# A wider pad beside right-hand tiles, a second raw weight buffer in the up projections, and modulation pieces in halves over eight slabs

## The chip, the cores and the metric

One core of a Trainium2 chip runs one program. The metric is the device time of the program in microseconds (us).

## What is computed

Two transformer blocks in float32 on 1024 tokens of width 1024. The first has a gated delta rule and a latent attention, the second a short convolution and a stick-breaking attention, whose inputs are modulated by a vector. Both end in a feed-forward part with 4096 hidden columns. What the change touches, from the reference:

```
h = rms_norm(x, ffn_pre_norm[l])
f = jnp.square(jax.nn.relu(h @ w_up[l])) @ w_down[l]
x = x + rms_norm(f, ffn_post_norm[l])
...
mod = c @ w_ada[l] + b_ada[l]
sh1, sc1, gt1, sh2, sc2, gt2 = jnp.split(mod, N_MOD, axis=-1)
h = modulate(rms_norm_2(x, g_pre_mix[l]), sh1, sc1)
proj = h @ w_in[l]
...
h2 = modulate(rms_norm_2(x, g_pre_mlp[l]), sh2, sc2)
ff = jnp.square(jax.nn.relu(h2 @ w_mlp_in[l])) @ w_mlp_out[l]
```

## The kernel before

Every product is made of three matmuls per contraction tile of 128: each operand is split into a high part (rounded, `w_hi`, made by ScalarE) and a low part (`w_lo`, the rest, made by VectorE), and high times high, high times low and low times high are summed in PSUM.

**The up projection** (`up_stage`, `ffn_up`, L1039) runs once per block, and is called stage 1 and stage 2 here. It works on 16 slabs of 256 hidden columns. A slab is a 2 by 2 block product in a form with seven products in place of eight; a product is 12 matmuls of 512 columns. The moving operand is a tile of activations, the stationary one a piece of weights. Two of the seven products use the activation quarters `hq` (left-hand tiles); the other five use `hq_t`, five tiles made from sums of quarters, which lie on the right-hand side of the memory. For the first 12 slabs (`LEAD`) the two `hq` products are made ahead, while the activations are still being normed, and parked in DRAM (`fx_dr`), so that such a lead slab has 5 products, 60 matmuls; the last four slabs have 84.

In a slab (L1060) SP loads 1 MB of weights into `w_raw`; it is the only buffer for raw weights, and the other stages use it too. VectorE makes four sums of weight quarters (`fws`, L1070), ScalarE and VectorE split `fws` and quarters of `w_raw` into two sets of `w_hi` and `w_lo` (L178, L179); there are two buffers of each, so both are in use in every slab. VectorE takes the products out of PSUM (L1095 to L1122: `fu2`, `fu3`, `f00`, `f11`, `f01`, `f10`), ScalarE squares them after a relu (L1050, L1051), VectorE makes five sums of the squares (`fs`, L1127, three buffers), and SP writes them to DRAM (L1043). ScalarE's queue writes two more. What `fs` holds is read back by the down projection.

**The modulation** (L1226 to L1277) computes `c @ w_ada` on VectorE in pieces of 512 columns: four loads of 512 KB on POOL's queue, two VectorE instructions for each (`ada_acc`, L1235 and L1237). Four pieces are worked off in stage 1, one `yield` per slab (`side(c)`), eight more in the first part of block 2.

**Memory.** Tiles with `side="right"` are stacked from the right-hand end. `edge` (L1512) is a pad, a tile that nothing uses, put there before `hq_t` (`between`, L1529) and before `h`, the activations of block 2 (L1561 to L1563). The right-hand end that the program may use lies 32 bytes below a multiple of 256 bytes. The addresses in this and the next section are those of the built programs.

The order of instructions on each engine comes from a scheduler; within `ffn_up` the products ahead have a high priority (L1131). An engine's instructions, and the DMAs of its queue, start in their order.

Of the kernel before, what the change touches and what calls it, by code (L numbers as in the profile page):

```python
# [8 lines left out]
F32 = mybir.dt.float32  # L9
# [8 lines left out]
P = 128  # L18
# [15 lines left out]
TAGS = {  # L34
# [5 lines left out]
}  # L40
# [25 lines left out]
def tile_two_blocks(ctx: ExitStack, tc: tile.TileContext, I, out):  # L66
# [5 lines left out]
    wp = ctx.enter_context(tc.tile_pool(name="wp", bufs=2))  # L72
# [966 lines left out]
    def ffn_up(hq, w_up, fl, fp, first, side):  # L1039
# [18 lines left out]
            return x  # L1058

        def slab(c, lead):  # L1060
            raw = wp.tile([P, 2112], F32, name="w_raw", tag="w_raw", bufs=1)[:, :2048]
            SP.dma_start(raw.rearrange("p (k n) -> p k n", k=8),
                         w_up[:, 256 * c:256 * c + 256].rearrange("(k p) n -> p k n", p=P))
            r4 = raw.rearrange("p (h k i n) -> p h i k n", h=2, k=4, i=2)
            (a11, a21), (a12, a22) = ([r4[:, h, i] for i in range(2)] for h in range(2))
            ws = fp.tile([P, 4, 4, P], F32, name="fws")
            s2, s3, s1, s4 = (ws[:, n] for n in range(4))
            for o, x, z, op in ((s1, a21, a22, ALU.add), (s2, s1, a11, ALU.subtract), (s3, a11, a21, ALU.subtract),
                                (s4, a12, s2, ALU.subtract)):
                DVE.tensor_tensor(out=o, in0=x, in1=z, op=op)  # L1070
            u = [[wp.tile([P, 2112], F32R, name=nm, tag=nm)[:, :2048].rearrange("p (s k n) -> p s k n", s=4, k=4)
                  for nm in ("w_hi", "w_lo")] for _ in range(2)]

            def halves_of(t, slots, v):
                split(t[0][:, slots], t[1][:, slots], v)

            def op(t, n):
                return [x[:, n] for x in t]

            if not lead:  # L1080
                halves_of(u[0], slice(2, 4), r4[:, :, 0])
            halves_of(u[0], slice(0, 2), ws[:, 0:2])
            halves_of(u[1], slice(0, 2), ws[:, 2:4])
            halves_of(u[1], 2, a22)
            if lead:
                x, f11 = (fp.tile([P, 512], F32, name=nm) for nm in ("fx", "f00"))
                for i, t in enumerate((x, f11)):
                    SP.dma_start(t, fx_dr[:, 512 * (2 * c + i):512 * (2 * c + i) + 512])
                q2 = f11
            else:  # L1090
                x = p1(fp, op(u[0], 2))
            q6 = mm_tile()
            product(q6, op(u[0], 0), "t2")
            u2 = fp.tile([P, 512], F32, name="fu2")
            DVE.tensor_tensor(out=u2, in0=x, in1=q6, op=ALU.add)  # L1095
            if not lead:
                q2 = mm_tile()
                product(q2, op(u[0], 3), "b21")
                f11 = fp.tile([P, 512], F32, name="f00")
            DVE.tensor_tensor(out=f11, in0=x, in1=q2, op=ALU.add)  # L1100
            square(f11)
            left(c, 2, f11, ACT)
            q7 = mm_tile()
            product(q7, op(u[0], 1), "t3")
            u3 = fp.tile([P, 512], F32, name="fu3")
            DVE.tensor_tensor(out=u3, in0=u2, in1=q7, op=ALU.add)
            q5 = mm_tile()
            product(q5, op(u[1], 0), "t1")
            f22 = fp.tile([P, 512], F32, name="f11")
            DVE.tensor_tensor(out=f22, in0=u3, in1=q5, op=ALU.add)  # L1110
            square(f22)
            left(c, 3, f22, ACT)
            q4 = mm_tile()
            product(q4, op(u[1], 2), "t4")
            f12 = fp.tile([P, 512], F32, name="f01")
            DVE.tensor_tensor(out=f12, in0=u3, in1=q4, op=ALU.subtract)
            square(f12)
            f21 = fp.tile([P, 512], F32, name="f10")
            DVE.tensor_tensor(out=f21, in0=u2, in1=q5, op=ALU.add)
            q3 = mm_tile()  # L1120
            product(q3, op(u[1], 1), "b22")
            DVE.tensor_tensor(out=f21, in0=f21, in1=q3, op=ALU.add)  # L1122
            square(f21)
            for i, x, z, o in ((4, f11, f12, ALU.add), (0, f11, f22, ALU.add), (6, f12, f22, ALU.subtract),
                               (1, f21, f22, ALU.add), (5, f21, f11, ALU.subtract)):
                t = fp.tile([P, 512], F32, name="fs")
                DVE.tensor_tensor(out=t, in0=x, in1=z, op=o)  # L1127
                left(c, i, t)


        with tc.high_priority(offset=100):  # L1131
            for c in range(LEAD):
# [3 lines left out]
                for i, (a, b) in enumerate(((a11, "b11"), (a12, "b21"))):  # L1136
                    acc = mm_tile()
# [85 lines left out]
        return res  # L1223


    def modulation_acc(i, pool):  # L1226

        acc = pool.tile([P, 512], F32, name="ada_acc")
        for q in range(4):
            raw = pool.tile([P, 2, 512], F32, name="ada_raw")  # L1230
            POOL.dma_start(raw, I["w_ada_2"][0][256 * q:256 * q + 256, 512 * i:512 * i + 512]
                           .rearrange("(k p) n -> p k n", p=P))
            for k in range(2):
                if q + k == 0:
                    DVE.tensor_scalar(acc, raw[:, 0, :], col(R_C), None, ALU.mult)  # L1235
                else:
                    DVE.scalar_tensor_tensor(out=acc, in0=raw[:, k, :], scalar=col(R_C + 2 * q + k), in1=acc,  # L1237
                                             op0=ALU.mult, op1=ALU.add)
        return acc

    def modulation_sum(i, acc, pool):
        row = pool.tile([P, 512], F32, name="f_r")[0:1, :]
        p = mm_tile()
        PE.matmul(p[0:1, :], ones[:, 0:1], acc, start=True, stop=True)
        ACT.copy(row, p[0:1, :])
        SP.dma_start(mod_raw[i // 2:i // 2 + 1, (i % 2) * 512:(i % 2) * 512 + 512], row)
# [18 lines left out]

    def modulation(pool, m0, m1):

        pend = None
        for i in range(2 * m0, 2 * m1):
            acc = modulation_acc(i, pool)  # L1270
            if pend is not None:
                modulation_sum(i - 1, pend, pool)
            pend = acc
            yield
        modulation_sum(2 * m1 - 1, pend, pool)
        modulation_columns(pool, m0, m1)
        yield  # L1277

# [176 lines left out]
    with sbuf("gc", 1) as gc:  # L1455
# [4 lines left out]
        with sbuf("hT1", 1) as hp:  # L1460
# [6 lines left out]
            right = ExitStack()  # L1467
# [43 lines left out]

    def edge(es, name):  # L1512

        es.enter_context(tc.tile_pool(name=name, bufs=1, side="right")).tile([P, 8], F32, name=name)

    def up_stage(n, w_out, src, mxp, mx_es, w_up, epi, tags, gains, side=lambda fp: lambda c: None):

# [24 lines left out]
    with ExitStack():  # L1542
        with banks(mm=6, tr=2):
# [7 lines left out]
            def side1(fp):  # L1551
# [7 lines left out]
                    t, xt, xn, junk, None, None, row=rows["grow"], tmp_pool=ep, put=put), spare=False),  # L1559
# [76 lines left out]
```

## Time and profile before

| | |
|---|---|
| median of 3 runs | 2800.58 us (2790.0 to 2802.42) |
| profiled execution | 2799.73 us, of which the span from its first to its last instruction is 2798.0 us |
| TensorE, share of the span with a matmul in flight | 95% |
| VectorE / ScalarE / GpSimd busy | 70% / 47% / 20% |
| TensorE clock granted, mean over the span | 0.985 |

Times within the execution are us from the span's start. Stage 1's slabs run from about 728 to 1010, stage 2's from about 2190 to 2455. A matmul of 512 columns is shown as lasting 0.39 us, but a new one starts about every 0.23 us, so the busy share of TensorE hides short waits; start times and counts show them.

### The profile page before, as it was taken

Reading aid. Unit: us, or ns where it says so; the run is one execution under the profiler, and the core shown is the slowest. Engines: PE = TensorE matmul, PEld = TensorE weight load, DVE = VectorE, ACT = ScalarE, POOL = GpSimd, SP = SyncE. Lnnn points to the kernel's source line nnn. Section 1 sums busy time; section 2 is a strip of 40 time slices with the busy share of each in tenths; the row PEclk is TensorE's granted clock in tenths of the full one; section 3 lists DMA queues with packets and bytes.
Section 4 is the critical chain, followed back from the end, with each engine's and each line's share of the span. In section 5 each row is a group of like instructions: output and inputs, shape, how many; then the busy total and the mean of one; then the engine's idle time right before and its main releaser. Section 6 shows DMA issues by size and latency. Waiting matters only on the chain. (4 is left out here: it accounts for less than half of the span.)

```text
span 2798.0 us, 39356 instructions
## 1 busy us (share of the span) xinstructions
PE 2658.9 (95%) x13801; PEld 2223.7 (79%) x13801; DVE 1957.6 (70%) x3614; ACT 1310.8 (47%) x2360; POOL 561.4 (20%) x568
## 2 busy tenths in 40 slices
PE   7899989999989999999999999998999989999996
PEld 7788879999766778777887788887798767878785
DVE  7668789858888765577765248777567778755566
ACT  4554666546544444344521146554268544443342
POOL 1242344300000022434211012111200000023412
PEclk9999999999999999999999999999999999999998
DMA  4286476356676587777574445343856566587785
GB/s 131 79 280 206 159 212 180 110 162 207 231 257 204 179 289 235 256 255 263 188 244 156 158 151 162 114 121 130 261 174 210 202 213 208 186 288 261 257 283 176
DMA packets 381500, 562.23 MB, mean 201 GB/s; under 512 B 39427, under 2 KB 215658, under 8 KB 381302
## 3 DMA queue, kind: packets, MB, share of 16 engines
q1 hardware_dynamic: 358262, 505.17, 55.0%
q10 hardware_dynamic: 16128, 29.37, 2.8%
q0 software_dynamic: 6912, 25.17, 2.8%
q8 instruction: 109, 1.79, 0.3%
q14 instruction: 89, 0.73, 0.1%
HBM read 408.83 MB, written 150.78 MB: 200 GB/s over the span
## 5 line engine op out<-in xcount | busy, mean ns | idle before, releaser
L173 PE MATMUL mm<-w_hi,df 128*128 128x512 f32 x1792 | 561.7, 394 | 13.8 <-ACT y L1197 5.7
L173 PE MATMUL mm<-hq_t,w_hi 128*128 128x512 f32 x1280 | 400.1, 401 | 26.3 <-ACT w_hi L178 24.0
L173 PEld LDWEIGHTS mm<-w_hi,df 128*128 128x128 f32 x1792 | 339.9, 190 | 88.7 <-ACT w_hi L178 7.3
L173 PE MATMUL mm<-w_lo,df 128*128 128x512 f32 x896 | 354.0, 395 | 10.9 <-DVE w_lo L179 10.8
L173 PEld LDWEIGHTS mm<-hq_t,w_hi 128*128 128x128 f32 x1280 | 240.3, 190 | 96.0 <-ACT w_hi L178 35.7
L173 PE MATMUL mm<-h_hi,w_hi 128*128 128x512 f32 x736 | 293.6, 399 | 0.0
L173 PE MATMUL mm<-h_lo,w_hi 128*128 128x512 f32 x736 | 292.4, 397 | 0.0
L173 PE MATMUL mm<-h_hi,w_lo 128*128 128x512 f32 x736 | 291.8, 397 | 0.0
L1170 POOL TENSOR_TENSOR dwr<-dwr 128x1024 f32<-128x1024 f32 x40 | 101.3, 2533 | 889.3 <-DMA dwr<-in_w_mlp_out 581.8
L173 PE MATMUL mm<-hq_t,w_lo 128*128 128x512 f32 x640 | 243.7, 398 | 8.1 <-DVE w_lo L179 8.0
L209 DVE TENSOR_TENSOR w_lo<-w_raw,w_hi 128x1024 fp32r<-128x1024 f32 (+1 forms) x138 | 170.7, 1259 | 92.7 <-ACT w_hi L203 91.7
L179 DVE TENSOR_TENSOR df<-dfr,df 128x1024 fp32r<-128x1024 f32 x112 | 155.3, 1397 | 85.3 <-ACT df L178 85.1
L203 ACT CAST w_hi<-w_raw 128x1024 fp32r<-128x1024 f32 (+1 forms) x138 | 138.8, 1047 | 158.1 <-PE mm L173 62.6
L173 PEld LDWEIGHTS mm<-w_lo,df 128*128 128x128 f32 x896 | 170.5, 190 | 51.9 <-DVE w_lo L179 16.7
L173 PE MATMUL mm<-w_hi,mixT 128*128 128x256 f32 x1024 | 183.5, 281 | 4.7 <-DVE m_sg L1439 2.0
L178 ACT CAST df<-dfr 128x1024 fp32r<-128x1024 f32 x112 | 116.5, 1051 | 120.3 <-PE mm L173 74.0
L179 DVE TENSOR_TENSOR w_lo<-dwr,w_hi 128x1024 fp32r<-128x1024 f32 x56 | 102.1, 1824 | 100.3 <-ACT w_hi L178 100.0
L173 PEld LDWEIGHTS mm<-h_hi,w_hi 128*128 128x128 f32 x736 | 138.3, 188 | 36.2 <-issue 6.3
L173 PEld LDWEIGHTS mm<-h_hi,w_lo 128*128 128x128 f32 x736 | 138.4, 188 | 29.7
L173 PEld LDWEIGHTS mm<-w_hi,mixT 128*128 128x128 f32 x1024 | 156.5, 188 | 6.7 <-ACT w_hi L203 4.0
L173 PEld LDWEIGHTS mm<-h_lo,w_hi 128*128 128x128 f32 x736 | 138.5, 188 | 29.1 <-issue 0.2
L173 PE MATMUL mm<-hq,w_hi 128*128 128x512 f32 x512 | 158.8, 391 | 0.0
(406 smaller groups left out, 5809.4 us busy)
## 6 DMA issues: line engine op xcount, KB each, us to landing
dfr<-fs SPq DMA_DIRECT2D x112, 512.0 KB
fs<-fs SPq DMA_DIRECT2D x160, 256.0 KB
w_raw<-in_w_in SPq DMA_DIRECT2D x32, 1024.0 KB
ada_raw<-in_w_ada POOLq DMA_DIRECT2D x48, 512.0 KB, 5.3
dwr<-in_w_down SPq DMA_DIRECT2D x48, 512.0 KB
w_raw<-in_w_down SPq DMA_DIRECT2D x48, 512.0 KB
dwr<-in_w_mlp_out SPq DMA_DIRECT2D x48, 512.0 KB
w_raw<-in_w_mlp_out SPq DMA_DIRECT2D x48, 512.0 KB
```

The costliest lines, as they stand in the source:

```text
L173: PE.matmul(ps, l, r, start=first and n == 0, stop=final and n == last)
L178: ACT.copy(hi, src)
L179: DVE.tensor_tensor(out=lo, in0=src, in1=r32(hi), op=ALU.subtract)
L203: ins = ACT.copy(wh[:, step * i:step * i + step], raw[:, step * i:step * i + step])
L209: DVE.tensor_tensor(out=wl[:, c], in0=raw[:, c], in1=r32(wh[:, c]), op=ALU.subtract)
L1170: POOL.tensor_tensor(out=a, in0=a, in1=b, op=ALU.subtract if sub else ALU.add)
```

## The change

`edge` becomes 224 bytes in place of 32. `hq_t` starts at byte 147200 in place of 147392, `h` of block 2 at 163584 in place of 163776: multiples of 256, where it was 192 bytes more than one. The tiles `hq`, `w_hi`, `w_lo` and block 1's `h` start at multiples of 256 in both kernels.

Odd slabs load their weights into a new tile `fraw`, even ones into `w_raw`. To make room for its 8 KB, `f01` and `f10` go: the results are made in place of `fu3` and `fu2`. `fs` has two buffers in place of three, `ada_raw` one in place of two in stage 1, `ada_acc` two in place of one. (The modulation of block 2 has pools of its own, as before.)

A piece of the modulation yields after its second load as well, and there the sum over partitions of the piece before is made. So a slab of stage 1 has half a piece, and four pieces take eight slabs; in block 2 half a piece goes with each call.

```
-    "fp": "fws fx*2 f00*2 fu2 fu3 f01 f10 f11 fs*3 ada_acc ada_raw*2 f_r",
+    "fp": "fws fraw fx*2 f00*2 fu2 fu3 f11 fs*2 ada_acc*2 ada_raw f_r",
...
         def slab(c, lead):
-            raw = wp.tile([P, 2112], F32, name="w_raw", tag="w_raw", bufs=1)[:, :2048]
+            if c % 2:
+                raw = fp.tile([P, 2048], F32, name="fraw")
+            else:
+                raw = wp.tile([P, 2112], F32, name="w_raw", tag="w_raw", bufs=1)[:, :2048]
...
-            f12 = fp.tile([P, 512], F32, name="f01")
+            f12 = u3
...
-            f21 = fp.tile([P, 512], F32, name="f10")
+            f21 = u2
...
-    def modulation_acc(i, pool):
+    def modulation_acc(i, pool, first, prev):
...
+            if q == 1:
+                if i > first:
+                    modulation_sum(i - 1, prev, pool)
+                yield
         return acc
...
         for i in range(2 * m0, 2 * m1):
-            acc = modulation_acc(i, pool)
-            if pend is not None:
-                modulation_sum(i - 1, pend, pool)
-            pend = acc
+            acc = yield from modulation_acc(i, pool, 2 * m0, acc)
             yield
...
-        es.enter_context(tc.tile_pool(name=name, bufs=1, side="right")).tile([P, 8], F32, name=name)
+        es.enter_context(tc.tile_pool(name=name, bufs=1, side="right")).tile([P, 56], F32, name=name)
```

Lines from L1062 on move by 3 to 7 (L1070 is L1073, L1127 is L1130, and so on).

The order that the scheduler makes also moves. First SP's queue at the start of stage 2's slabs, before:

```order
L1062 DMA w_raw_22739<-in_w_mlp_in_2 128x8x256
L1088 DMA f00_22757<-fx_dr_98 128x512
L1088 DMA f00_22880<-fx_dr_98 128x512
L1062 DMA w_raw_22862<-in_w_mlp_in_2 128x8x256
L1088 DMA fx_23002<-fx_dr_98 128x512
L1043 DMA fs0_99<-fs_22850 128x512
L1062 DMA w_raw_22985<-in_w_mlp_in_2 128x8x256
```

and now:

```order
L1065 DMA w_raw_22693<-in_w_mlp_in_2 128x8x256
L1065 DMA fraw_22814<-in_w_mlp_in_2 128x8x256
L1065 DMA w_raw_22935<-in_w_mlp_in_2 128x8x256
L1091 DMA fx_22952<-fx_dr_98 128x512
L1043 DMA fs0_99<-fs_22802 128x512
L1065 DMA fraw_23056<-in_w_mlp_in_2 128x8x256
L1043 DMA fs4_103<-fs_22799 128x512
```

The load for the second slab follows the first at once, and each later load stands a slab earlier than it did.

Then VectorE in a lead slab of stage 2 (`mm` is a product in PSUM), before:

```order
L1095 TENSOR_TENSOR fu2_23142<-fx_23125,mm_23129 128x512
L1127 TENSOR_TENSOR fs_23093<-f00_23003,f01_23071 128x512
L1127 TENSOR_TENSOR fs_23099<-f01_23071,f11_23053 128x512
L1127 TENSOR_TENSOR fs_23105<-f10_23075,f00_23003 128x512
L1106 TENSOR_TENSOR fu3_23161<-fu2_23142,mm_23148 128x512
L1070 TENSOR_TENSOR fws_23233<-w_raw_23231 128x512 x2
L1070 TENSOR_TENSOR fws_23233<-fws_23233,w_raw_23231 128x512
L1070 TENSOR_TENSOR fws_23233<-w_raw_23231,fws_23233 128x512
L1127 TENSOR_TENSOR fs_23102<-f10_23075,f11_23053 128x512
```

and now:

```order
L1130 TENSOR_TENSOR fs_23044<-f00_22953,f11_23003 128x512
L1130 TENSOR_TENSOR fs_23041<-f00_22953,fu3_22988 128x512
L1130 TENSOR_TENSOR fs_23050<-fu2_22969,f11_23003 128x512
L1130 TENSOR_TENSOR fs_23047<-fu3_22988,f11_23003 128x512
L179 TENSOR_TENSOR w_lo_23187<-fws_23179,w_hi_23186 128x1024
L179 TENSOR_TENSOR w_lo_23187<-w_raw_23177,w_hi_23186 128x512
L1073 TENSOR_TENSOR fws_23300<-fraw_23298 128x512 x2
L1130 TENSOR_TENSOR fs_23053<-fu2_22969,f00_22953 128x512
```

Four of the five sums follow each other, on two buffers, and the fifth comes after four instructions on weights; the weights of the next slab are worked on right behind those of this one.

Last, VectorE in a slab of stage 1 with the modulation, now:

```order
L1130 TENSOR_TENSOR fs_9994<-f00_9903,f11_9953 128x512
L179 TENSOR_TENSOR w_lo_10157<-fws_10151,w_hi_10156 128x1024
L1130 TENSOR_TENSOR fs_9991<-f00_9903,fu3_9938 128x512
L1240 SCALAR_TENSOR_TENSOR ada_acc_10006<-ada_raw_10145,vec_107,ada_acc_10006 128x512
L1130 TENSOR_TENSOR fs_10000<-fu2_9919,f11_9953 128x512
L1240 SCALAR_TENSOR_TENSOR ada_acc_10006<-ada_raw_10145,vec_107,ada_acc_10006 128x512
L1130 TENSOR_TENSOR fs_9997<-fu3_9938,f11_9953 128x512
L179 TENSOR_TENSOR w_lo_10159<-fws_10151,w_hi_10158 128x1024
L179 TENSOR_TENSOR w_lo_10159<-w_raw_10149,w_hi_10158 128x512
L1130 TENSOR_TENSOR fs_10003<-fu2_9919,f00_9903 128x512
```

The two L1240 are the halves of one load. Four instructions on the modulation fall to a slab, where a slab with a piece had eight; they and `w_lo` now stand between the sums.

## Rows read from the trace of the kernel before

**Rows 1.** The page's first part: busy us of the span, instructions.
```profile
PE 2658.9 (95%) x13801; PEld 2223.7 (79%) x13801; DVE 1957.6 (70%) x3614; ACT 1310.8 (47%) x2360; POOL 561.4 (20%) x568
```

**Rows 2.** Windows: stretch, us, busy by engine (count), PEclk, DMA share, GB/s.
```profile
728.00:867.00 139.00, 121.22 (x473) 88.83 (x472) 113.00 (x171) 55.92 (x86) 11.77 (x16) 0.95 0.69 230
867.00:927.00 60.00, 57.02 (x240) 44.26 (x239) 51.78 (x79) 28.86 (x44) 0.00 (x0) 1.00 0.68 220
927.00:1010.00 83.00, 83.00 (x358) 66.68 (x357) 59.41 (x85) 37.55 (x54) 4.10 (x2) 1.00 0.55 189
2190.00:2376.00 186.00, 172.41 (x721) 133.87 (x721) 145.82 (x219) 81.73 (x127) 0.00 (x0) 1.00 0.63 208
2376.00:2455.00 79.00, 79.00 (x343) 63.78 (x342) 58.71 (x82) 38.80 (x57) 5.24 (x3) 1.00 0.56 193
1380.00:1890.00 510.00, 508.95 (x2588) 420.65 (x2586) 312.56 (x507) 203.82 (x412) 77.56 (x152) 1.00 0.50 160
```

**Rows 3.** Waits in 2190 to 2376: us in total, times, longest.
```profile
DVE fws L1070 <- DMA w_raw<-in_w_mlp_in: 38.2, 12, 3.8
PE mm L173 <- ACT w_hi L178: 9.3, 10, 1.6
```

**Rows 4.** Timeline of one slab of stage 2: start, us, instruction, idle before.
```profile
2222.52 0.68 DVE L179 TENSOR_TENSOR w_lo<-w_raw,w_hi 128x512 fp32r<-128x512 f32 x1
2223.23 0.38 SPq L1062 DMA_DIRECT2D w_raw<-in_w_mlp_in  x1
2229.66 1.29 DVE L1070 TENSOR_TENSOR fws<-w_raw 128x512 f32<-128x512 f32 x2 [3.46 <-DMA w_raw<-in_w_mlp_in]
2231.64 1.06 ACT L178 CAST w_hi<-fws 128x1024 fp32r<-128x1024 f32 x1 [8.01 <-DVE fws L1070]
2233.88 1.21 DVE L179 TENSOR_TENSOR w_lo<-fws,w_hi 128x1024 fp32r<-128x1024 f32 x1
2235.14 0.50 PE L173 MATMUL mm<-hq_t,w_lo 128*128 128x512 f32 x1 [1.15 <-DVE w_lo L179]
```

**Rows 5.** Waits in 728 to 867.
```profile
POOL ada_raw L1231 <- DVE ada_acc L1237: 88.6, 13, 10.8
DVE fws L1070 <- DMA w_raw<-in_w_up: 14.6, 7, 3.6
PE mm L173 <- ACT w_hi L178: 13.0, 6, 4.7
```

**Rows 6.** Timeline of TensorE in four unbroken runs of 512-column matmuls.
```profile
2172.91 0.39 PE L173 MATMUL mm<-hq,w_lo 128*128 128x512 f32 x1
...
2177.67 0.39 PE L173 MATMUL mm<-hq,w_lo 128*128 128x512 f32 x1
...
298.88 0.39 PE L173 MATMUL mm<-h_hi,w_hi 128*128 128x512 f32 x1
...
302.96 0.39 PE L173 MATMUL mm<-h_hi,w_hi 128*128 128x512 f32 x1
...
840.83 0.39 PE L173 MATMUL mm<-hq_t,w_lo 128*128 128x512 f32 x1
...
843.86 0.40 PE L173 MATMUL mm<-hq_t,w_lo 128*128 128x512 f32 x1
...
1558.09 0.39 PE L173 MATMUL mm<-h_lo,w_hi 128*128 128x512 f32 x1
...
1558.79 0.40 PE L173 MATMUL mm<-h_lo,w_hi 128*128 128x512 f32 x1
```

**Rows 7.** Timeline of VectorE: sums of squares, and a wait for a buffer.
```profile
865.76 1.89 DVE L1127 TENSOR_TENSOR fs<-f,f 128x512 f32<-128x512 f32 x3
...
869.93 0.69 DVE L1127 TENSOR_TENSOR fs<-f,f 128x512 f32<-128x512 f32 x1 [0.49 <-DMA fs<-fs]
```

**Rows 8.** The tile ada_raw in 720 to 1000: ns min/median/max, and its loads.
```profile
L1237 DVE SCALAR_TENSOR_TENSOR ada_acc<-ada_raw,vec,ada_acc x28: 732/744/750, 737.7 to 850.8; 128x512 f32<-128x512 f32 x28
DMA to landing us min/median/max: 3.9/6.1/8.7
```

More of the change, by code (lines that the diff above doesn't have):

```diff
@@ L1266, in modulation @@
     def modulation(pool, m0, m1):
-        pend = None
+        acc = None
         for i in range(2 * m0, 2 * m1):
-            acc = modulation_acc(i, pool)
-            if pend is not None:
-                modulation_sum(i - 1, pend, pool)
-            pend = acc
+            acc = yield from modulation_acc(i, pool, 2 * m0, acc)
             yield
-        modulation_sum(2 * m1 - 1, pend, pool)
+        modulation_sum(2 * m1 - 1, acc, pool)
         modulation_columns(pool, m0, m1)
```

## The prediction, made before the changed kernel ran

> **What bounds the kernel now.** TensorE has a matmul in flight for 2658.9 of 2798.0 us [rows 1], but a matmul is shown as 0.39 us long and a new one starts each 0.23 us, so this share hides waits. Two other views are needed.
>
> The first is the timeline of unbroken runs, where the spacing of start times is what a matmul really takes. In the `hq` run 21 matmuls lie between the two rows: (2177.67 - 2172.91) / 21 = 0.2267 us. In block 1's `h` 18 lie between: 4.08 / 18 = 0.2267. In the `hq_t` run 13: 3.03 / 13 = 0.2331. In block 2's `h` three: 0.70 / 3 = 0.2333 [rows 6]. The clock is full in all of them. The reader is to see that `h` is fast in one block and slow in the other, with the same columns and the same instructions: what differs is where the moving tile starts. The fast ones start at a multiple of 256 bytes, the slow ones 192 bytes past one. The difference is 6.6 ns, 2.8% of a matmul.
>
> The second is the windows by stage [rows 2]. In stage 2, 2190 to 2376 holds 721 matmuls, 12 lead slabs of 60: 186 / 12 = 15.5 us each, where 60 matmuls at 0.2333 take 14.0. So 1.5 us of a slab is waiting. VectorE is busy for 145.82 us there, 12.2 us per slab, so it isn't the limit. It idles 38.2 us for `w_raw`, in each of 12 slabs [rows 3]. The timeline shows the loop [rows 4]: the last reader of `w_raw` starts at 2222.52, SP issues the next load at 2223.23, VectorE gets the weights only at 2229.66 after idling 3.46 us, `w_hi` comes at 2231.64, `w_lo` at 2233.88, and TensorE waits 1.15 us for it. The load, 6.4 us, lies in a chain from slab to slab because there is one raw buffer.
>
> In stage 1, 728 to 867 holds 473 matmuls, 7.9 slabs: 139 / 7.9 = 17.6 us each. The modulation adds VectorE work, TensorE waits up to 4.7 us for `w_hi` [rows 5], and the clock that it is granted averages 0.95 [rows 2]: a tenth of the stretch is at 1.2 GHz in place of 2.4, which costs 0.05 x 139 = 7 us. The next four slabs take 60 / 4 = 15.0 us. The rest, 927 to 1010, has TensorE in flight all the time, as have 2376 to 2455 and, but for 1 us, block 2 from 1380 to 1890.
>
> **The change part by part.**
>
> *The pad, block 2.* 1728 matmuls of the program have `h` as the moving operand there, at 6.6 ns: 11.4 us. Of these, in the new order, 690 stand between matmuls of the stick-breaking attention, whose own chain could set the end instead; 1038 don't: 6.9 us. The bounds are 6.9 and 11.4; TensorE is in flight for 508.95 of 510 us [rows 2], which is nearest to the second, and I take 10. Another 384 matmuls have `h` as the stationary operand; no run isolates that, so within 6.6 ns either way, 2.5 us, and I take nothing.
>
> *The pad, last four slabs of both stages.* TensorE is the limit there [rows 2]: 240 matmuls with `hq_t` in each stage, 1.6 us each, 3.2 together.
>
> *The second raw buffer, lead slabs of stage 2.* The load of slab c+1 can land while slab c is worked on, which takes out the 3.46 us that VectorE idled [rows 4]; TensorE's 1.15 us wait at the end of that chain goes with it. What is late next: TensorE needs 60 x 0.2267 = 13.6 us, VectorE 12.2. The buffers that were given away cost something here. Four sums of squares now follow each other on two buffers, so the third waits until the first is written out. The trace has that wait with three buffers: sums start at 865.76, 0.60 apart, the first is done at 866.4, and the fourth starts when its write has landed, at 869.93 [rows 7], 3.5 us. By that the third sum would idle 3.5 - 0.6 = 2.9 us; the fifth stands behind 2.9 us of other work and would idle little. From below it is nothing, if writes land within 0.6 us or VectorE would have waited for a product anyway. Bounds per slab: 13.6 and 12.2 + 2.9 = 15.1. The row's write was issued behind a 1 MB load, and in the new order the load is queued after the four sums, so I take 2.0: 14.2 us. That saves 1.3 x 12 = 15.6 us (bounds 4.8 and 22.8).
>
> *The results in place* (`f12` in `fu3`, `f21` in `fu2`): the next slab's `fu2` waits until two sums are done, about 3 us after the last product; the next product ends 12 x 0.2267 = 2.7 us after it, and there are six PSUM banks. No cost, hidden behind a bank or two of products ahead. Without that cover it is 0.5 us per slab, inside the bounds.
>
> *Stage 1, first eight slabs.* VectorE has 12.2 us, as in stage 2, plus four modulation instructions of at most 0.74 [rows 8], 3.0: 15.2 us, above TensorE's 13.6. VectorE becomes the limit. With the wait for a sum's buffer at 0 to 2.9 this gives 15.2 to 18.1; modulation and `w_lo` now stand between the sums, so I take 1.0: 16.2. One `ada_raw` buffer means load, two instructions, load, two instructions: 2 x (6.1 + 1.5) = 15.2 us at the median landing [rows 8], just as long, so it costs nothing unless loads are late. The 88.6 us for which POOL waited for VectorE to free a buffer [rows 5] stay harmless. The weights' waits and with them the stretches at 1.2 GHz go. (17.6 - 16.2) x 8 = 11.2 us (bounds -4 and 19.2).
>
> *Stage 1, next four slabs.* 15.0 to 14.2: 3.2 us (bounds 0 and 5.6).
>
> *The modulation in block 2* spreads over twice as many calls and ends before the attention begins in the new order; VectorE is busy 61% there [rows 2]. Nothing.
>
> Sum: 10 + 3.2 + 15.6 + 11.2 + 3.2 = 43.2 us off the profiled execution's 2799.73, which is 0.85 us below the median: **2756.5**, so 2757. All bounds at their best: 13.9 + 3.2 + 22.8 + 19.2 + 5.6 = 64.7, so 2735. All at their worst: 4.4 + 3.2 + 4.8 - 4 + 0 = 8.4, so 2791.
>
> The Trainium skill, "SBUF — State Buffer", Specifications (TRN2), gives the memory's lines as 16 bytes and has a penalty for crossing into a new one. Both starts of `hq_t` are multiples of 16, so by that page the pad would change nothing, and the sum would be that of the third rival. Rows 6 speak against it: 0.2267 and 0.2333 at starts that the page's rule treats alike.
>
> **The rivals.**
>
> *The waits only move* (0.18). Writes of the sums land as late as in rows 7 and the modulation's loads take 7.3 us, between the median of 6.1 and the longest of 8.7 [rows 8]: lead slabs 15.1, the first eight 2 x (7.3 + 1.5) = 17.6, unchanged. 10 + 3.2 + 4.8 + 0 = 18, so 2782. For it: 3.5 us was measured. Against: with three buffers that wait cost VectorE 0.49 us there, and the new loads of 1 MB stand behind the sums.
>
> *TensorE alone is the limit* (0.12), everything else hidden: the best bounds but for 16.0 us per slab in the first eight: 13.9 - 2.5 + 3.2 + 22.8 + 12.8 + 5.6 = 55.8, so 2744. Against it: VectorE at 12.2 of 13.6 us has little room.
>
> *The pad does nothing* (0.04), if it isn't the start that makes matmuls 6.6 ns longer but something else in which the two places differ. Then block 2 and the last slabs give 0, lead slabs stop at 14.0 at best, and at about 14.3 with the same waits: 1.2 x 12 + 11.2 + 2.8 = 28.4, so 2771.
>
> *Slower* (0.04): the two `fs` buffers put the writes of all five sums in series. With two waits of L - 0.6 in place of one, a lead slab takes 12.2 + 2 (L - 0.6); at L = 3.5 that is 18.0 us, and 21.0 with modulation. Against 15.5, 17.6 and 15.0: 2.5 x 12 + 3.4 x 8 + 3 x 4 = 69 us lost, 13 won, so 2856. It decides above L = 2.25, where a lead slab reaches 15.5. Against it: the new order never has five sums in a row in the slabs shown; the fifth has four instructions ahead of it.
>
> **How the numbers follow.** The forecast has 0.60, the rivals 0.38, and 0.02 is for the reordering of other parts. A measurement of this kernel can tell about 0.5% from no change, 14 us: faster means below 2786.6. The forecast, the second and third rival and three quarters of the first lie there: 0.89. The first rival's upper end makes 0.07 for the same, the last one and a bit 0.04 for slower. The range runs from the best bounds, 2736, to just inside the worst, 2786, and leaves out the last rival and the ends of the others.
>
> **What would show it.** The spacing in `hq_t` and block 2's `h` should be 0.2267 (the pad). VectorE should idle next to nothing for `w_raw` and `fraw` in front of `fws`, and TensorE have no wait over 1 us for `w_hi` in stage 2. Stage 2's lead slabs should take about 14.2 us, stage 1's first eight about 16.2 with a granted clock of 0.99 or more, and new idle time should stand in front of `fs` (L1130), released by its own writes, up to 2 us per slab. The prediction is wrong if spacing stays at 0.2333, if that idle time passes 3 us per slab, or if VectorE idles for `ada_raw` in each slab of stage 1.

## The result and the profile after

The changed kernel took 2819.7 us (median of 5 runs, 2815.06 to 2828.66) against 2799.53 for the kernel before: a ratio of 1.0083, 95% interval 1.0055 to 1.011. It is slower, by 20 us, where 43 us less was forecast, and it lies above the range. The profiled execution took 2828.66 us (span 2827.0), 9 us above the median, so its parts are told against each other and not summed to the median.

The stages first. Stage 1 and stage 2 are taken from the first matmul with `hq_t` to the first matmul of the down projection (operand `df`); the first 480 matmuls with `hq_t` are eight slabs, the first 720 the twelve lead slabs. All times are us, from the start times of matmuls in the two profiled executions.

| | before | after |
|---|---|---|
| stage 1 | 280.9 | 302.9 |
| of it the first eight slabs | 142.9 | 157.4 |
| stage 2 | 265.9 | 275.2 |
| of it the lead slabs | 188.8 | 200.1 |
| down projection of stage 1 and block 2 up to the stick-breaking attention | 631.6 | 626.3 |
| from the out projection of block 2 to stage 2 | 167.6 | 173.4 |
| span | 2798.0 | 2827.0 |

Stage 1 lost 22 us and stage 2 lost 9; the rest is -2 together. The page's first part (busy us of the span, instructions) hardly shows it against [rows 1]:

```profile
PE 2654.5 (94%) x13801; PEld 2240.7 (79%) x13801; DVE 1971.4 (70%) x3614; ACT 1309.2 (46%) x2360; POOL 564.5 (20%) x568
```

The stages are seen in its windows (stretch, us, busy by engine with counts, granted clock, DMA share, GB/s): the first eight slabs and the next four of stage 1 and its rest, then stage 2's lead slabs and its rest. They answer to [rows 2].

```profile
728.00:886.00 158.00, 124.79 (x488) 97.98 (x489) 122.51 (x181) 56.73 (x89) 11.78 (x16) 0.87 0.67 215
886.00:949.00 63.00, 58.99 (x255) 46.91 (x255) 50.43 (x75) 29.68 (x47) 0.00 (x0) 1.00 0.58 196
949.00:1031.00 82.00, 76.43 (x324) 62.68 (x325) 59.20 (x80) 36.31 (x53) 4.79 (x2) 0.96 0.50 172
2210.00:2410.00 200.00, 178.02 (x734) 143.12 (x733) 152.21 (x220) 86.17 (x130) 0.00 (x0) 0.95 0.56 194
2410.00:2485.00 75.00, 73.80 (x326) 60.73 (x325) 58.86 (x80) 35.55 (x52) 4.80 (x2) 1.00 0.50 176
```

The reader is to see that no engine is the limit in the lead slabs: VectorE is busy 152.21 of 200 us and TensorE's clock, 1.00 before, is 0.95. In the first eight slabs of stage 1 the clock is 0.87, so about a quarter of that stretch ran at 1.2 GHz and the rest at 2.4.

What they wait for, in stage 2 from 2210 to 2411 (us in total, times, longest), which answers to [rows 3]:

```profile
DVE fs L1130 <- DMA fs<-fs: 29.7, 17, 4.4
...
PEld mm L173 <- DVE fu L1098: 22.3, 7, 4.4
PE mm L173 <- DVE fu L1098: 19.3, 7, 3.9
```

and in stage 1's lead slabs from 728 to 945, which answers to [rows 5]:

```profile
POOL ada_raw L1234 <- DVE ada_acc L1240: 117.0, 15, 9.5
...
PE mm L173 <- DVE fu L1098: 35.8, 5, 12.7
...
DVE fs L1130 <- DMA fs<-fs: 21.8, 14, 3.5
...
DVE ada_acc L1240 <- DMA ada_raw<-in_w_ada: 11.9, 8, 4.5
```

The waits for `w_raw` of [rows 3] are gone, as forecast. In their place VectorE waits for the writes of its own sums, and TensorE for `fu`, the first thing that VectorE does for the next slab. The second is what the forecast had at nothing. One slab of stage 2 shows how the two hang together (timeline of VectorE, then of SP's queue, whose merged row of five writes is followed by the fourth of them alone, then of TensorE):

```profile
2246.53 0.68 DVE L1130 TENSOR_TENSOR fs<-f,f 128x512 f32<-128x512 f32 x1
...
2248.33 0.68 DVE L1130 TENSOR_TENSOR fs<-f,fu 128x512 f32<-128x512 f32 x1
...
2250.79 1.23 DVE L179 TENSOR_TENSOR w_lo<-fws,w_hi 128x1024 fp32r<-128x1024 f32 x1 [0.45 <-ACT w_hi L178]
2254.29 1.38 DVE L1130 TENSOR_TENSOR fs<-fu,f 128x512 f32<-128x512 f32 x2 [2.28 <-DMA fs<-fs]
2257.77 0.69 DVE L1130 TENSOR_TENSOR fs<-fu,f 128x512 f32<-128x512 f32 x1 [2.10 <-DMA fs<-fs]
...
2260.12 0.68 DVE L1098 TENSOR_TENSOR fu<-fx,mm 128x512 f32<-128x512 f32 x1
...
2246.64 0.38 SPq L1065 DMA_DIRECT2D w_raw<-in_w_mlp_in  x1
2247.24 11.58 SPq L1043 DMA_DIRECT2D fs<-fs  x5
...
2255.70 0.32 SPq L1043 DMA_DIRECT2D fs<-fs  x1
...
2256.53 0.39 PE L173 MATMUL mm<-hq_t,w_lo 128*128 128x512 f32 x1
2260.86 1.22 PE L173 MATMUL mm<-hq_t,w_hi 128*128 128x512 f32 x2 [3.94 <-DVE fu L1098]
2261.87 0.63 PE L173 MATMUL mm<-hq_t,w_lo 128*128 128x512 f32 x1
2262.30 1.05 PE L173 MATMUL mm<-hq_t,w_hi 128*128 128x512 f32 x2
```

The load of 1 MB is issued at 2246.64, just ahead of the first sum's write at 2247.24. The third sum needs the first sum's buffer and gets it at 2254.29, 7.05 us after that write was issued. The fifth follows the fourth at once and needs the buffer of just that one (the addresses and waits of the built program show it): the fourth's write was issued at 2255.70 and had landed by 2257.77, after 2.07 us with no load just ahead. Since `f21` lies in the tile of `fu2`, and the fifth sum reads it, the next slab's `fu2` can't be written before: it starts at 2260.12, behind the fifth sum and two more instructions on `w_lo`. TensorE, whose last matmul had started at 2256.53, is released by it (`fu2` takes a product out of PSUM) and starts again at 2260.86, a gap of 4.1 us. From 2260.42 it is granted 1.2 GHz for 3.4 us, where a matmul takes 0.43 us: 2261.87 to 2262.30. In the lead slabs of stage 2 TensorE waits for `fu` seven times, 19.3 us in all, and at the end of four of these waits the granted clock falls to 1.2 GHz.

The pad did to the spacing what was forecast. Two unbroken runs of the kernel after, which answer to [rows 6]: 54 matmuls with `hq_t` lie between the first two rows, 27 with `h` of block 2 between the last two.

```profile
2279.79 0.40 PE L173 MATMUL mm<-hq_t,w_lo 128*128 128x512 f32 x1
...
2292.05 0.39 PE L173 MATMUL mm<-hq_t,w_lo 128*128 128x512 f32 x1
...
1502.40 0.39 PE L173 MATMUL mm<-h_lo,w_hi 128*128 128x512 f32 x1
...
1508.52 0.39 PE L173 MATMUL mm<-h_lo,w_hi 128*128 128x512 f32 x1
```

12.26 / 54 = 0.2270 us and 6.12 / 27 = 0.2267, where it was 0.2331 and 0.2333.

### The profile page after: what moved, and what is told of

It is laid out like the page before. It is cut to its first block, busy times and chain, and to the rows that moved or that the text cites. A ratio compares the mean times of both kernels' runs of the same rounds, so it can differ in the third digit from the quotient of the medians.

```text
span 2827.0 us, 39450 instructions
## 1 busy us (share of the span) xinstructions
PE 2654.5 (94%) x13801; PEld 2240.7 (79%) x13801; DVE 1971.4 (70%) x3614; ACT 1309.2 (46%) x2360; POOL 564.5 (20%) x568
## 4 chain that ended last, share of the span: by engine, by line
PE 25%; DMA 17%; DVE 10%; ACT 4%; POOL 4%; issue 3%; SPq 1%; POOLq 0%; DVEq 0%; ACTq 0%
PE mm L173 21%; DMA w_raw<-in_w_down 3%; DVE w_lo L179 3%; DMA w_raw<-in_w_mlp_out 3%; POOL w_raw L1173 3%; DMA fs<-fs 2%; ACT w_hi L178 2%; DMA dwr<-in_w_mlp_out 1%; DMA dwr<-in_w_down 1%; PE po L906 1%; DVE w_lo L209 1%; POOL dwr L1173 1%; PE tr L898 1%; DMA mrg<-m_sg 1%; DMA m_sg<-sig 1%
## 5 line engine op out<-in xcount | busy, mean ns | idle before, releaser
L173 PE MATMUL mm<-hq_t,w_hi 128*128 128x512 f32 x1280 | 411.0, 406 | 68.4 <-DVE fu L1098 61.9
L173 PEld LDWEIGHTS mm<-hq_t,w_hi 128*128 128x128 f32 x1280 | 249.4, 196 | 131.8 <-DVE fu L1098 37.7
L173 PE MATMUL mm<-hq_t,w_lo 128*128 128x512 f32 x640 | 253.5, 402 | 1.6 <-DVE w_lo L179 1.6
L1173 POOL TENSOR_TENSOR w_raw<-w_raw 128x1024 f32<-128x1024 f32 x40 | 109.0, 2725 | 580.1 <-DMA fs<-fs 392.2
L173 PEld LDWEIGHTS mm<-w_lo,df 128*128 128x128 f32 x896 | 169.7, 189 | 49.0 <-DVE w_lo L179 14.2
L179 DVE TENSOR_TENSOR df<-dfr,df 128x1024 fp32r<-128x1024 f32 x112 | 147.1, 1324 | 56.5 <-ACT df L178 56.3
```

The costliest lines, as they stand in the source:

```text
L173: PE.matmul(ps, l, r, start=first and n == 0, stop=final and n == last)
L179: DVE.tensor_tensor(out=lo, in0=src, in1=r32(hi), op=ALU.subtract)
L1173: POOL.tensor_tensor(out=a, in0=a, in1=b, op=ALU.subtract if sub else ALU.add)
```

## The experiments

The theory after this: the sums' waits and the results in place make the loss together. Two buffers make the sums wait for their writes, and the results in place put the next slab's `fu2`, and so TensorE's banks, behind those waits. The rivals: one of the two alone is the whole loss; the modulation's single `ada_raw` buffer is; the pad costs something; the second raw buffer gains nothing to begin with. All runs, with stage times from their profiled executions as in the first table:

| run | median us | ratio to before, 95% interval | stage 1 (first eight slabs) | stage 2 (lead slabs) |
|---|---|---|---|---|
| changed kernel | 2819.7 | 1.0083 [1.0055, 1.011] | 302.9 (157.4) | 275.2 (200.1) |
| pad_only | 2787.59 | 0.998 [0.9963, 0.9997] | 283.9 (145.8) | 265.3 (189.5) |
| no_pad | 2832.06 | 1.0134 [1.0115, 1.0153] | 306.3 (158.4) | 273.4 (197.4) |
| sums4 | 2800.3 | 1.0024 [1.0011, 1.0037] | 290.4 (133.2) | 273.1 (176.5) |
| apart | 2797.59 | 1.0006 [0.999, 1.0021] | 291.0 (132.0) | 273.2 (171.5) |
| stage2_room | 2761.95 | 0.9894 [0.9853, 0.9934] | 281.3 (143.0) | 243.4 (167.9) |
| halves_only | 2782.3 | 0.995 [0.9936, 0.9964] | 275.6 (130.1) | 265.3 (189.2) |
| all_room | 2790.6 | 0.9978 [0.9965, 0.9992] | 291.2 (122.8) | 265.7 (169.5) |
| room_two_sums | 2765.83 | 0.9896 [0.9874, 0.9918] | 282.0 (143.9) | 249.5 (174.0) |
| room_in_place | 2769.53 | 0.9892 [0.987, 0.9914] | 283.6 (144.6) | 252.3 (177.2) |
| room_both | 2793.13 | 1.0002 [0.9984, 1.0021] | 284.8 (147.1) | 269.4 (195.9) |
| room_halves | 2759.98 | 0.9875 [0.9858, 0.9893] | 276.3 (130.1) | 241.5 (168.0) |
| early | 2749.27 | 0.9828 [0.9814, 0.9843] | 269.4 (124.2) | 243.6 (168.1) |

The runs of the kernel before beside them had medians of 2794.4 (pad_only to apart), 2797.49 (stage2_room to all_room), 2797.26 (room_two_sums, room_in_place, room_halves, early) and 2796.42 (room_both). The profiled executions of pad_only and halves_only lay 9 and 8 us above the medians of their runs, so their stage times are rather high.

**pad_only**, the kernel before with the wide pad:

```
-    ...tile([P, 8], F32, name=name)
+    ...tile([P, 56], F32, name=name)
```

> The kernel before with the pad of 224 bytes alone. If the start of the moving tile sets the spacing, hq_t and block 2's h go from 0.2333 to 0.2267 us. Block 2 and the last four slabs of both stages then give 10 + 3 us, the lead slabs little, since the raw weights' load still sets their 15.5 us: about 2785. If lead slabs follow TensorE after all, 10 + 13 us: 2777. If the pad is worth nothing in time: 2800.

Measured: 0.998, which is 5.6 us of 2794.4 (0.8 to 10.3). The lead slabs don't gain (189.5 against 188.8 us), since the load in series sets their pace. In block 2 the stretch from the 193rd to the 1921st matmul with `h` took 433.7 us in place of 440.7, so 7.0 less.

**no_pad**, the changed kernel with the narrow pad:

```
-    ...tile([P, 56], F32, name=name)
+    ...tile([P, 8], F32, name=name)
```

> The changed kernel with the old pad of 32 bytes. If the pad's gain and the slabs' loss add up, this is the changed kernel plus 12 to 15 us, 2832 to 2835. If the slabs are bound by VectorE and TensorE waits anyway, only block 2 and the last slabs lose: plus 10 to 13. If the pad is itself behind the loss, this is at or below 2800.

Measured: 1.0134 where the changed kernel has 1.0083, and the intervals don't meet. By the ratios the pad is a gain of some 14 us (0.0051 of 2794.4) there too, by the medians 12; it isn't the cause of the loss.

**sums4**, the changed kernel with four buffers for the sums. The two added ones are the lead's tiles `fx` and `f00` in the pool `fl`; `sums()` hands out the four in turn:

```
-                t = fp.tile([P, 512], F32, name="fs")
+                t = sums()
```

> The changed kernel with four buffers for the sums of squares in place of two (the lead's two tiles, idle then, take every other sum). Theory W, the sums' wait for their own writes is what costs: VectorE's idle time for fs, 33 us in stage 1 and 37 us in stage 2 of the changed kernel, goes to under 5 each, TensorE's wait for fu goes with it, and the kernel falls by 35 to 50 us, to 2770 to 2785. Theory P, the results made in place of fu2 and fu3 are what costs: the wait for fs goes, TensorE's wait for fu stays above 40 us in all, and the time falls by less than 15 us.

**apart**, the changed kernel with the results out of `fu3` and `fu2`, in the same two tiles; the sums keep two buffers:

```
-            f12 = u3
+            f12 = fl.tile([P, 512], F32, name="fx")
...
-            f21 = u2
+            f21 = fl.tile([P, 512], F32, name="f00")
```

> The changed kernel with two buffers for the sums, but f12 and f21 in tiles of their own (the lead's two). Theory W: VectorE still idles some 70 us for fs, the time falls by less than 15 us. Theory P: the next slab's fu2 and fu3 need not wait for the sums, TensorE's wait for fu falls from 85 us to under 25, and the time falls by 35 to 50 us though VectorE still waits for fs.

Measured: either one brings the lead slabs of stage 2 from 200.1 to 176.5 and 171.5 us and the first eight of stage 1 from 157.4 to 133.2 and 132.0. So each part of the pair is needed for the loss in the slabs. But the ratios of the whole are 1.0024 and 1.0006, and neither theory's forecast of the time came in either run, since much of what was gained there is given back: stage 2's rest took 102 us in apart and 97 in sums4 in place of 75. The waits of apart in 2206 to 2480 show a new one, once, where the down projection begins:

```profile
PE mm L173 <- ACT w_hi L178: 28.6, 1, 28.6
```

**stage2_room**, the kernel before with the pad, and the second raw buffer in stage 2 alone. Stage 2 has no modulation in its slabs, so there is room for it with nothing given up: `f01`, `f10` and three `fs` stay.

```
+    "fp2": "fws fraw fx*2 f00*2 fu2 fu3 f01 f10 f11 fs*3",
...
+            if two and c % 2:
+                raw = fp.tile([P, 2048], F32, name="fraw")
+            else:
```

> The pad, and the second raw buffer in stage 2 alone, where the modulation's tiles are not needed: f01 and f10 stay, the sums have three buffers. Stage 1 as before. Theory W with P (what was given up costs, not the second buffer): VectorE no longer idles for w_raw, lead slabs of stage 2 go from 15.7 to about 14.0 us, and the kernel is 15 to 22 us faster than the one with the pad alone, 2767 to 2773. Theory L (the earlier 1 MB loads crowd out the writes and the next stage's loads): stage 2 stays above 262 us, and the kernel is within 5 us of the pad alone, at 2783 to 2793.

Measured: 0.9894, faster than both kernels and than the 2767 to 2773 of the first theory; the second, by which stage 2 stays above 262 us, is out. The lead slabs took 167.9 us where pad_only has 189.5: 14.0 us each. Their window:

```profile
2178.40:2346.30 167.90, 165.31 (x724) 135.21 (x723) 148.80 (x222) 82.81 (x128) 0.00 (x0) 1.00 0.68 232
```

The wait for a sum's buffer in it:

```profile
DVE fs L1131 <- DMA fs<-fs: 6.9, 5, 1.6
```

TensorE is in flight for 165.31 of 167.9 us at full clock: it is the limit now, and the second raw buffer is worth 21.6 us in the lead slabs of stage 2.

**halves_only**, the kernel before with the pad and the modulation in halves (`ada_raw` one buffer, `ada_acc` two):

```
-    "fp": "fws fx*2 f00*2 fu2 fu3 f01 f10 f11 fs*3 ada_acc ada_raw*2 f_r",
+    "fp": "fws fx*2 f00*2 fu2 fu3 f01 f10 f11 fs*3 ada_acc*2 ada_raw f_r",
```

> The pad, and the modulation in halves over eight slabs with one ada_raw and two ada_acc; one raw buffer, all else as before. If the halves help stage 1 (VectorE work spread, no slab with a whole piece), its first eight slabs fall by 5 to 12 us against the pad alone, 2776 to 2783. If one ada_raw buffer makes VectorE wait for loads as in the changed kernel (13 us there), it is even or up to 8 us slower, 2788 to 2796.

Measured: 0.995 against pad_only's 0.998, some 8 us less, though the intervals just touch; stage 1 is 8.3 us shorter. The first eight slabs take 130.1 us (145.8 in pad_only), the next four 70.0 (60.3): part of the modulation's work is moved into them. With the halves, one `ada_raw` buffer is no net loss.

**all_room**, the changed kernel with three `fs`, the results in `fl`'s tiles and a row `f_r` of half the size, in both stages:

```
-    "fp": "fws fraw fx*2 f00*2 fu2 fu3 f11 fs*2 ada_acc*2 ada_raw f_r",
+    "fp": "fws fraw fx*2 f00*2 fu2 fu3 f11 fs*3 ada_acc*2 ada_raw f_r",
```

> The changed kernel with three buffers for the sums and f12 and f21 apart in both stages (the lead's two tiles, and a row of the modulation of half the size, make the room). Theories W and P together: VectorE's waits for fs fall under 15 us in all and TensorE's for fu under 10, stage 1 takes 265 to 272 us and stage 2 248 to 255, and the kernel takes 2758 to 2770. Theory L: the slabs are fast, but the wait of 20 us or more where the down projection begins, seen with the results apart, stays in both stages, 2785 to 2797.

Measured: 0.9978, 2790.6 us: not the 2758 to 2770 of the first two theories, but what theory L has, a wait where the down projection begins, in both stages. The first eight slabs of stage 1 are the fastest of all (122.8), yet the stage took 291.2 us. Its end (timeline of TensorE, VectorE, SP's queue and POOL):

```profile
994.38 0.39 PE L173 MATMUL mm<-hq_t,w_lo 128*128 128x512 f32 x1
1015.34 2.07 PE L173 MATMUL mm<-w_hi,df 128*128 128x512 f32 x4 [20.57 <-ACT w_hi L178]
...
1001.88 0.69 DVE L1130 TENSOR_TENSOR fs<-f,f 128x512 f32<-128x512 f32 x1 [1.17 <-DMA fs<-fs]
...
1002.60 0.32 SPq L1043 DMA_DIRECT2D fs<-fs  x1
...
1003.48 13.97 SPq L1169 DMA_DIRECT2D dwr<-in_w_down  x4
...
1011.87 2.34 POOL L1173 TENSOR_TENSOR dwr<-dwr 128x1024 f32<-128x1024 f32 x1 [12.44 <-DMA dwr<-in_w_down]
```

The down projection's weights `dwr` are loaded only when the last sum is done, and TensorE stands for 20.6 us. In the built programs `dwr` begins at byte 97024 and is 8 KB long; `fl`'s `fx` and `f00` lie at 97024 and 99072. What was put there in the last slab is what `dwr` waits for. This was the cost of my own edit, in all_room as in sums4 and apart; the changed kernel doesn't have it.

The four corners in stage 2, all else as in stage2_room. **room_two_sums**:

```
-    "fp2": "fws fraw fx*2 f00*2 fu2 fu3 f01 f10 f11 fs*3",
+    "fp2": "fws fraw fx*2 f00*2 fu2 fu3 f01 f10 f11 fs*2",
```

> Stage 2 as in stage2_room (12 lead slabs in 167.9 us, 2761.95 us in all), but the sums have two buffers in place of three; the results keep tiles of their own. Theory (only both together stall TensorE: the sums wait for their writes, and the next slab's fu2 and fu3 stand behind them because the results lie in their tiles): VectorE idles some 2 us per slab for its own writes, but TensorE has no waits over 2 us; lead slabs 168 to 173 us, 2762 to 2767 in all. Rival (the two buffers alone are the whole loss): lead slabs about 200 us as in the changed kernel, 2794 in all.

**room_in_place**:

```
-            f12 = fp.tile([P, 512], F32, name="f01")
+            f12 = u3 if two else fp.tile([P, 512], F32, name="f01")
...
-            f21 = fp.tile([P, 512], F32, name="f10")
+            f21 = u2 if two else fp.tile([P, 512], F32, name="f10")
```

> Stage 2 as in stage2_room, but the results are made in place of fu3 and fu2; three buffers for the sums. Theory (both together): lead slabs 170 to 180 us, 2764 to 2774 in all, as the sums rarely wait. Rival (the results in place are the whole loss, since fu2 and fu3 stand behind the five sums whether these wait or not): lead slabs about 200 us, 2794 in all.

**room_both**, the two edits together:

> The fourth corner in stage 2: two buffers for the sums and results in place, all else as in stage2_room (stage 1 as before the change). Against stage2_room's 167.9 us in 12 lead slabs, two buffers alone gave 174.0 and results in place alone 177.2. Theory (each buffer covers for the other, and the two together are the changed kernel's loss): lead slabs 195 to 205 us, waits of 3 to 4 us of TensorE for fu2 or fu3 in every other slab with the clock at its lower level behind them, 2788 to 2798 in all. Rival (the two losses add, 6 + 9 us, and the rest of the changed kernel's loss in stage 2 has another cause, for instance the later end of stage 1): lead slabs about 183 us, 2774 to 2780 in all.

Measured: 167.9 us for the lead slabs with neither, 174.0 with two buffers, 177.2 with the results in place, 195.9 with both; 2761.95, 2765.83, 2769.53 and 2793.13 us in all. By themselves they cost 6.1 and 9.3 us of stage 2, and in the ratios (0.9896 and 0.9892 against 0.9894) nothing that could be told; together they cost 28.0. The windows of the lead slabs, first with two buffers, then in place, then both:

```profile
2175.20:2349.20 174.00, 170.09 (x735) 138.44 (x736) 153.81 (x226) 89.29 (x132) 0.00 (x0) 0.99 0.68 226
```

```profile
2182.50:2359.70 177.20, 170.95 (x732) 137.65 (x732) 153.41 (x222) 86.76 (x131) 0.00 (x0) 0.99 0.68 220
```

```profile
2183.10:2379.00 195.90, 173.62 (x733) 140.16 (x734) 153.33 (x223) 84.72 (x130) 0.00 (x0) 0.97 0.58 200
```

The waits of room_both in its window:

```profile
DVE fs L1131 <- DMA fs<-fs: 24.0, 18, 2.3
...
PE mm L174 <- DVE fu L1099: 20.9, 7, 3.6
```

VectorE's busy time is the same in all three. With the two buffers alone no wait of TensorE for `fu` is among the long ones; with the results in place alone there are short ones (stage 2 from 2180 to 2420):

```profile
PE mm L174 <- DVE fu L1099: 4.6, 8, 2.4
```

With both TensorE waits for `fu` seven times and 20.9 us, as in the changed kernel (7 times, 19.3). The rival by which the two losses add, 183 us, is out.

**room_halves**, halves_only and stage2_room together (no new line):

> Pad, halves of modulation pieces in stage 1 (one raw buffer there), second raw buffer with room in stage 2. If the gains add: 2761.95 - (2787.59 - 2782.3) = 2756.7, between 2752 and 2761. Rival (halves gain nothing once stage 2 is fast, or the gain was another run's chance): 2762 or more.

Measured: 2759.98, inside the expected 2752 to 2761; but stage2_room's 2761.95 is only 2 us above, and the intervals of the two overlap, so the halves' gain on top isn't shown by the time in all. By stage it is: stage 1 took 276.3 us against 281.3.

**early**, stage 2 as in stage2_room, stage 1 as in all_room but with the results in `fl`'s tiles only up to slab 13:

```
-            f12 = fl.tile([P, 512], F32, name="fx")
+            f12 = fp.tile([P, 512], F32, name="f01") if two else fl.tile([P, 512], F32, name="fx") if c < 14 else u3
...
-            f21 = fl.tile([P, 512], F32, name="f00")
+            f21 = fp.tile([P, 512], F32, name="f10") if two else fl.tile([P, 512], F32, name="f00") if c < 14 else u2
```

> Stage 2 as in stage2_room; stage 1 as in all_room, but from slab 14 on the results are made in place, so that the last reader of the two tiles of the lead, over which the down projection's first weights (dwr) are laid, comes two slabs earlier. Theory (the 20.7 us gap of TensorE where the down projection begins in all_room is dwr's load waiting for results and their sums in those two tiles): the gap is under 4 us, stage 1 takes 265 to 272 us (291.2 in all_room, 281.3 in stage2_room), 2743 to 2753 in all. Rival (the gap comes from the queue of SP behind late writes of the sums, whatever tile dwr lies on): the gap stays at about 20 us, stage 1 about 290, 2768 to 2775 in all.

Measured: 0.9828, 2749.27 us, the fastest of all runs and inside the expected 2743 to 2753. TensorE goes from `hq_t` to `df` with no gap:

```profile
999.09 0.39 PE L174 MATMUL mm<-hq_t,w_lo 128*128 128x512 f32 x1
999.31 0.39 PE L174 MATMUL mm<-w_hi,df 128*128 128x512 f32 x1
```

So the gap was the tile that `dwr` lies on, not SP's queue. Stage 1 took 269.4 us, 33.5 less than in the changed kernel, with the same second raw buffer, the same halves and the same single `ada_raw` buffer.

## Why the prediction was wrong

**The step that failed** is the term for the results in place, put at "No cost, hidden behind a bank or two of products ahead", and with it the way in which the wait for a sum's buffer was put into a slab. The wait itself was taken as 2.0 us per slab; the trace has 29.7 / 12 = 2.5. That is a small error. The large one was to add it to VectorE's 12.2 us, compare 14.2 with TensorE's 13.6, and take the larger. That holds for two engines that run beside each other with slack between them. The slack was PSUM's banks, and the results in place took it away: `fu2`, which frees a bank, stood behind the last sum. Then TensorE stood while VectorE waited for its writes, and a lead slab took 200.1 / 12 = 16.7 us with neither of them busy for more than 14.8. The prediction had `fu2` wait "until two sums are done, about 3 us after the last product"; but the second of those two is the fifth sum, and in the slab shown `fu2` starts 13.6 us after the first one. The prediction named the cover (the banks) and what it would cost to lose it, "0.5 us per slab". room_both against room_two_sums says 21.9 / 12 = 1.8 us per slab. The two were priced one by one, and each alone is indeed cheap (0.5 and 0.8 us per slab); the two together were never priced. Nor was the clock behind new waits: of the 32.2 us that the lead slabs take more than in stage2_room, 19.3 are TensorE's waits for `fu`, and the lower clock (0.95 of 200 us) is up to 10 more, an estimate from the two windows.

By parts, the first eight slabs of stage 1 lost 14.5 us in the profiled executions where 11.2 were to be won, and the lead slabs of stage 2 lost 11.3 where 15.6 were to be won; most of the miss is there.

Two details of the wait were wrong as well. "The fifth stands behind 2.9 us of other work and would idle little": it idled 2.10 us in the slab shown, the third 2.28, since there the fifth has no instruction between itself and the fourth. And "the load is queued after the four sums": in that slab the load of 1 MB was issued 0.6 us ahead of the first of the five writes, which then took 7.05 us.

**The rival on the slower side** had this mechanism in half: two waits in series, deciding above a landing of 2.25 us, to which 0.04 was given. The landings shown are 2.07 and 7.05 us, one on each side. Its case was weakened by "four instructions ahead" of the fifth sum, read from the order of one slab, which doesn't hold for the slab shown and tells nothing of how long a write takes. Its price, 2856, was too high: VectorE waited 17 times in twelve slabs, not 24. The Trainium skill, "SBUF — State Buffer", the section on the DMA setup-cost knee, fits a transfer's time as 2 us plus its bytes over 436 GB/s; for 256 KB that is an estimate of 2.6 us, over the rival's 2.25, and the skill says itself that this fit overstates at middle sizes. The trace agrees with that: 2.07 was measured with no load just ahead.

**The second raw buffer** was right and undersized: where nothing was given up for it, a lead slab takes 14.0 us (forecast 14.2) and the twelve save 21.6 us (forecast 15.6, bounds 4.8 to 22.8). The waits for raw weights are gone in the changed kernel too.

**Stage 1, first eight slabs:** 157.4 / 8 = 19.7 us where 16.2 was forecast. With room (early) it is 15.5, close to the 15.2 that was worked out for VectorE, though part of the modulation then falls into the next four slabs; all twelve took 203.4 us before, 220.6 in the changed kernel and 196.0 in early. That one `ada_raw` buffer "costs nothing unless loads are late" failed with the rest: VectorE waited 13.2 us for its loads, ten times (the row shown in the part on the result has eight of them). In early, with the same buffer, it is 7.8 us, five times, so part of these waits follows from the others: POOL issues the next load when VectorE has used the last one. But they are in the chain too. The longest wait of TensorE for `fu` in stage 1 ends behind two of them, which stand ahead of the last sum:

```profile
856.06 0.75 DVE L1240 SCALAR_TENSOR_TENSOR ada_acc<-ada_raw,vec,ada_acc 128x512 f32<-128x512 f32 x1 [2.46 <-DMA ada_raw<-in_w_ada]
...
863.74 0.75 DVE L1240 SCALAR_TENSOR_TENSOR ada_acc<-ada_raw,vec,ada_acc 128x512 f32<-128x512 f32 x1 [4.53 <-DMA ada_raw<-in_w_ada]
...
866.14 0.69 DVE L1130 TENSOR_TENSOR fs<-fu,f 128x512 f32<-128x512 f32 x1
...
868.61 0.68 DVE L1098 TENSOR_TENSOR fu<-fx,mm 128x512 f32<-128x512 f32 x1
...
869.44 1.19 PE L173 MATMUL mm<-hq_t,w_hi 128*128 128x512 f32 x2 [12.71 <-DVE fu L1098]
```

With the results in place, and by this order, a late load of the modulation reaches TensorE as well; no run has that by itself. The lower clock is a follow-on: it fell at TensorE's waits, and about 41 us of these eight slabs ran at 1.2 GHz, 14 before. sums4 and apart show that the pair is needed for the loss here too (133.2 and 132.0 us); how the rest divides between the sums, the results and the modulation wasn't tried by itself.

**Stage 1, next four slabs:** 14.2 us forecast, 63.2 / 4 = 15.8 measured, and 17.5 in halves_only. The forecast took it that the modulation ends with the eighth slab. In halves_only a part runs into the next four; in the changed kernel the slow first eight leave only its last sum and what follows that, and the window from 886 to 949 has the waits of stage 2 again: VectorE 9.5 us for `fs`, TensorE 3.3 for `fu`.

**The pad:** right in its mechanism, too large in its sum. The spacing fell to 0.227 us, but 13.2 us were forecast for it outside the lead slabs and pad_only gained 5.6 (0.8 to 10.3). A part of the difference may be the clock: the runs of pad_only have a mean granted clock of 0.982, those of the kernel before beside them 0.985, which over the span is some 7 us of full clock, an estimate from these two; no run takes that apart. Block 2 gave 7.0 us where 10 was taken; about four in ten of the matmuls between those of the stick-breaking attention still have a spacing of 0.231 us or more. The Trainium skill's rule of 16-byte lines ("SBUF — State Buffer", Specifications), by which the pad would do nothing, disagrees with these rows.

**Of the items that would show it wrong** the first, a spacing of 0.2333, did not come. The second, more than 3 us per slab in front of `fs`, came nearly (2.5). The third, idling for `ada_raw` in each slab of stage 1, came in seven of the eight slabs with modulation. None of the items was the idle time of TensorE in front of `fu`, which was the decisive one.

Left open: the stretch from block 2's out projection to stage 2 is 5.8 us longer in the changed kernel, and 3 to 9 us longer in all but pad_only (1.5); no run took that apart.

## What to carry to other kernels

Buffers that are given up are to be priced together, not one by one: ask for each wait which other engine's cover it uses, and whether another edit of the same change takes that cover away. An engine's waits may be added to its work and compared with another engine's only where there are buffers between the two that let them drift. Before a tile is reused for something that lives longer, look at what is laid over it in the next stage: two slabs less of use there were worth 20 us here.

## What was not expected of the hardware

The start of the stationary operand counts too, and not always in the same direction. 256-column matmuls with `h` as the stationary operand became slower when `h` moved to a multiple of 256 bytes. Before, 27 matmuls lie between these two rows, 3.18 / 27 = 0.1178 us:

```profile
1431.99 0.28 PE L173 MATMUL mm<-w_hi,h_lo 128*128 128x256 f32 x1
...
1435.17 0.28 PE L173 MATMUL mm<-w_hi,h_lo 128*128 128x256 f32 x1
```

After, 21 lie between these, 2.52 / 21 = 0.1200:

```profile
1440.02 0.28 PE L173 MATMUL mm<-w_hi,h_lo 128*128 128x256 f32 x1
...
1442.54 0.28 PE L173 MATMUL mm<-w_hi,h_lo 128*128 128x256 f32 x1
```

There are 384 of them, so it is 1 us. The pad alone does it: the median spacing is 0.120 us in pad_only and 0.118 in no_pad.

A write of 256 KB held up VectorE until 2.07 us after its issue in one case and until 7.05 us in another, where a load of 1 MB had been issued 0.6 us earlier on the same queue. In the lead slabs of stage 2 of the changed kernel, eleven of the seventeen waits for a sum's buffer ended 2.05 to 2.14 us after the issue, the others 2.4 to 7.05 us.
